# A new order of pieces in a cross-covariance attention kernel: nine stores held behind the last V load, K^T Q copies on ScalarE, last store in halves

## Chip, cores, metric

One core of a Trainium2 chip. The metric is the device time of one execution in microseconds (us). Times of before and after are medians of several runs; the profile is that of one execution. A ratio of two kernels is the mean time of one's fast runs over the mean of the other's fast runs of the same rounds, so it is not quite the ratio of the quoted medians.

## The reference

Q, K and V have the shape (8, 12, 512, 64) in float32: 96 heads of 512 tokens and 64 features.

```python
Q_norm = Q / (np.linalg.norm(Q, axis=-2, keepdims=True) + 1e-10)   # norm over the tokens
K_norm = K / (np.linalg.norm(K, axis=-2, keepdims=True) + 1e-10)
attn = np.einsum('bhnd,bhne->bhde', Q_norm, K_norm)                # 64x64 per head
attn = softmax(attn, axis=-1)
return np.einsum('bhnd,bhde->bhne', V, attn)
```

The three inputs are 37.75 MB and the output is 12.58 MB: 96 transfers of 0.5 MB.

## The kernel before

Four heads are a unit (24 units), two units a pair (12 pairs). The work is cut into pieces with short names that the text uses: `lq`, `lk`, `lv` load Q, K, V of a unit; `cq` casts Q or K to bf16 on DVE; `gr` multiplies [Q|K] with itself on PE (64 matmuls, one PSUM buffer); `sq` takes the squares out of it and `kq` copies K^T Q; `rd`, `sc`, `lg`, `ex`, `nm` make the attention matrix of a pair; `cv` casts V, `vt` transposes it on PE, `vc` copies the transpose out of PSUM; `ou` is the last product, `oc` its copy out of PSUM, `st` the store.

The program sorts these pieces itself, before it emits them. Each engine then runs its instructions in that fixed order, whatever arrives first. The sorting uses a duration and a rank that are written beside each piece:

```python
class Order:
    HOP, SLACK, QUEUE, FLIGHT = 0.15, 0.25, 8, 2.0
    def run(self):
        ...   # again and again: of the pieces that could begin first, emit the one of lowest rank
# a few of the pieces: key, {engine: booked us}, after, behind, rank
piece(("gr", u), {"PE": 1.6}, [("cq", u, 0), ("cq", u, 1), back("sq", u, 1)], [], 2, grams, u)
piece(("sq", u), {"DVE": 1.30}, [("gr", u), back("sc", s, NB["sm"])], [back("sq", u, 1)], 1, squares, u)
piece(("lv", v), {"DMA": X}, [back("cv", v, NB["v"])], [back("lv", v, 1)], v_at(v), load_v, v)
piece(("st", s, i), {"DMA": X}, [("oc", s, 2 * i), ("oc", s, 2 * i + 1)], order, v_at(2 * s + i) + ST_LAG, store, s, i)
```

```python
def grams(u):                     # PE: 64 weight loads and 64 matmuls
    g = gram[u] = ps_g.tile([128, HU, 512], F32, name="gram")
    for t in range(T):            # T = 16
        for h in range(HU):       # HU = 4
            x = qkb[u][32 * h:32 * (h + 1), t, :]
            nc.tensor.matmul(g[:, h, 0:2 * D], x, x, start=(t == 0), stop=(t == T - 1))

def squares(u):                   # DVE: squares twice, then the copy of K^T Q
    ...
    nc.vector.tensor_copy(kq[s][k], g[k, :, q])

def vtrans(s, k):                 # PE: one half of a pair's transposes
    for c in range(2):
        for j in range(J // 2):
            for r in range(2):
                t = J * c + k * (J // 2) + j
                nc.tensor.transpose(ps[r * D:(r + 1) * D, c, j, :], vb[2 * s + r][:, t, :], identb)
```

All loads and stores are issued in order by one queue (SP).

## Time and profile before

| | before |
|---|---|
| time, median | 135.4 us (135.18 to 135.93) |
| span of the profiled execution | 133.0 us |
| busy: PE, DVE, ACT, POOL | 83.4, 94.5, 64.9, 56.1 us |
| PE instructions in the profile | 2496 matmuls and 2496 weight loads |
| rate of the transfers until 110 us | 408 to 411 GB/s |

The prediction below shows the slices, stretches and waits. Two more lines of the page matter later. I did not use them for the prediction. The first belongs to the table of transfer queues (packets, MB, share): it is the queue that brings instructions, not data. The second is from the waits (total us, times, longest): PE stood still in the middle of its product while nothing that the profile knows was missing ("issue").

```profile
q8 instruction: 19, 0.31, 0.9%
```

```profile
PE gram L170 <- issue: 8.2, 6, 2.0
```

### The profile page before, as it was taken

The page shows a single profiled execution, that of the slowest core. Times are in us where ns is not written, and L with a number is a line of the kernel's source. Part 1 is how long each engine was busy: PE and PEld are TensorE (multiplying, and loading weights), DVE is VectorE, ACT ScalarE, POOL GpSimd, SP SyncE. Part 2 cuts the span into 40 slices and gives each one's busy share as a digit, 9 for nine tenths or more (in the row PEclk, how much of TensorE's full clock was granted, in tenths as well). Part 3 has the DMA queues.
Part 4 walks back from the last instruction along what each step waited for, and adds up shares of the span by engine and source line. Part 5 has one row for each costly group of instructions (what it writes and reads, how often), then busy time and mean ns, then how long its engine had stood idle before and what let it go on. Part 6 is the DMA issues. An engine that isn't in the chain of part 4 may idle for free.

```text
span 133.0 us, 5673 instructions
## 1 busy us (share of the span) xinstructions
PE 83.4 (63%) x2496; PEld 70.0 (53%) x2496; DVE 94.5 (71%) x186; ACT 64.9 (49%) x164; POOL 56.1 (42%) x55
## 2 busy tenths in 40 slices
PE   0145587585669944666859957459745956486550
PEld 0134486464457833654749845457634845485330
DVE  2477958899799469667754787467987679879800
ACT  0000056555632957155552885464857475269570
POOL 3000642869527328373066059064361378172000
PEclk9999999999655799777555699855999599959955
DMA  4999999999999999999999999999999999972976
GB/s 143 394 424 413 406 410 405 409 408 411 402 406 412 409 411 412 411 410 416 405 414 405 421 408 406 410 418 405 409 416 407 417 411 392 338 288 87 373 278 225
DMA packets 16921, 50.70 MB, mean 381 GB/s; under 512 B 1536, under 2 KB 1536, under 8 KB 16896
## 3 DMA queue, kind: packets, MB, share of 16 engines
q1 hardware_dynamic: 16896, 50.34, 95.9%
q8 instruction: 19, 0.31, 0.9%
q14 instruction: 6, 0.05, 0.1%
HBM read 37.75 MB, written 12.58 MB: 378 GB/s over the span
## 4 chain that ended last, share of the span: by engine, by line
DMA 41%; PE 19%; DVE 14%; issue 9%; ACT 8%; POOL 4%; SPq 1%; DVEq 1%; POOLq 1%; ACTq 0%
DMA v<-in_V_dram 15%; DMA qk<-in_K_dram 12%; PE gram L170 9%; DMA qk<-in_Q_dram 8%; DMA out_dram<-so 7%; PE po L250 4%; ACT vt L135 4%; DVE scr L180 4%; DVE qkb L158 3%; PE vps L231 3%; POOL r L194 3%; PE lg L203 2%; ACT so L135 2%; DVE so L137 2%; DVE kq L185 2%
## 5 line engine op out<-in xcount | busy, mean ns | idle before, releaser
L170 PE MATMUL gram<-qkb 32*128 32x128 bf16 x1536 | 37.7, 263 | 26.3 <-DVE qkb L158 15.0
L170 PEld LDWEIGHTS <-qkb 32*128 32x128 bf16 x1536 | 31.1, 117 | 31.5 <-DVE qkb L158 17.1
L194 POOL TENSOR_TENSOR r<-n,mhalf 128x8 f32<-128x8 f32 x12 | 22.3, 1858 | 42.4 <-DVE n L189 38.1
L158 DVE CAST qkb<-qk 128x1024 bf16<-128x1024 f32 x48 | 34.8, 761 | 7.4 <-DMA qk<-in_Q_dram 6.4
L135 ACT COPY vt<-vps 128x1024 bf16<-128x1024 bf16 (+1 forms) x26 | 28.2, 1089 | 13.0 <-PE vps L231 9.6
L139 POOL TENSOR_SCALAR vb<-v 128x1024 bf16<-128x1024 f32 x22 | 24.7, 1126 | 20.5 <-DMA v<-in_V_dram 20.2
L180 DVE SCALAR_TENSOR_TENSOR scr<-gram,eye 64x256 f32<-64x256 f32 x48 | 20.2, 422 | 17.7 <-PE gram L170 17.1
L135 ACT COPY so<-po 128x512 f32<-128x512 f32 x41 | 23.0, 592 | 17.3 <-PE po L250 17.1
L250 PE MATMUL po<-ab,vt 128*64 128x128 bf16 x384 | 21.6, 256 | 11.3 <-ACT vt L135 7.6
L250 PEld LDWEIGHTS <-vt 128*64 128x64 bf16 x384 | 15.7, 130 | 15.9 <-ACT vt L135 9.2
L210 ACT ACTIVATE ex<-lg,r 128x64 f32<-128x64 f32 x48 | 14.4, 313 | 15.9 <-PE lg L204 15.9
L231 PE MATMUL vps<-identb,vb 128*64 128x128 bf16 x384 | 20.1, 261 | 2.9 <-issue 1.8
L231 PEld LDWEIGHTS <-vb 128*64 128x64 bf16 x384 | 16.3, 137 | 4.3 <-issue 2.3
L203 PE MATMUL lg<-eye,kqs 64*64 64x64 f32 x96 | 10.3, 264 | 4.9 <-POOL kqs L196 4.9
L203 PEld LDWEIGHTS lg<-eye,kqs 64*64 64x64 f32 x96 | 8.4, 169 | 6.8 <-POOL kqs L196 5.9
L219 DVE TENSOR_TENSOR ab<-ex,rinv 64x256 bf16<-64x256 f32 x24 | 10.7, 446 | 0.6
L204 PE MATMUL lg<-eye,kqs 64*64 64x64 f32 x96 | 10.3, 264 | 0.0
L185 DVE COPY kq<-gram 64x256 f32<-64x256 f32 x24 | 10.1, 419 | 0.3
L210 ACT ACT_TABLE_LOAD x1 | 1.3, 1283 | 18.2 <-PE lg L204 18.2
L210 ACT ACTIVATION_READ_ACCUMULATOR ex<-lg,r 128x1 f32 x48 | 9.8, 205 | 0.0
L189 DVE TENSOR_REDUCE n<-scr 128x8 f32<-128x512 f32 x12 | 8.2, 687 | 0.4
L196 POOL TENSOR_TENSOR kqs<-kq,r 128x256 f32<-128x256 f32 x12 | 8.0, 669 | 0.9
(15 smaller groups left out, 23.2 us busy)
## 6 DMA issues: line engine op xcount, KB each, us to landing
qk<-in_Q_dram SPq DMA_DIRECT2D x24, 512.0 KB, 10.1
qk<-in_K_dram SPq DMA_DIRECT2D x24, 512.0 KB, 10.1
v<-in_V_dram SPq DMA_DIRECT2D x24, 512.0 KB, 10.1
out_dram<-so SPq DMA_DIRECT2D x24, 512.0 KB, 8.4
```

What stands on the lines that cost most here:

```text
L135: nc.scalar.copy(o, i)
L139: nc.gpsimd.tensor_scalar(out=o, in0=i, scalar1=1.0, scalar2=0.0, op0=ALU.mult, op1=ALU.add)
L158: nc.vector.tensor_copy(qkb[u][:, :, y * D:(y + 1) * D], qk32[u][:, y])
L170: nc.tensor.matmul(g[:, h, 0:2 * D], x, x, start=(t == 0), stop=(t == T - 1))
L180: nc.vector.scalar_tensor_tensor(out=scr[s][half, HU * (x ^ r):HU * (x ^ r) + HU], in0=g[half, :, half], scalar=1e-20, in1=eye2[half, None ...
L185: nc.vector.tensor_copy(kq[s][k], g[k, :, q])
L194: nc.gpsimd.tensor_tensor(out=t_, in0=n2, in1=mhalf, op=ALU.pow)
L203: nc.tensor.matmul(l[LO, h, :], kqs[s][HI, h, :], eye2[HI])
L210: nc.scalar.activation(e[:, h, :], lg[s][:, h, :], AF.Exp, scale=r8[s][:, h:h + 1], accum_out=z[:, h:h + 1])
L219: nc.vector.tensor_tensor(out=a[half, :, half], in0=e[half], in1=ri[half, :, None].to_broadcast([D, HU, D]), op=ALU.mult,)
L231: nc.tensor.transpose(ps[r * D:(r + 1) * D, c, j, :], vb[2 * s + r][:, t, :], identb)
L250: nc.tensor.matmul(po[s, x][e * D:(e + 1) * D, j].rearrange("p r d -> p (r d)"), w, ab[s][:, h, :])
```

## The change

The intent: the transfers are full until 110 us and then run dry, because stores that wait for outputs stand in front of the last V loads. So put Q and K loads earlier, issue all V loads without being held, and leave nine stores and the two halves of the last one to be drained at the end. To make the Q/K part faster, the K^T Q copy becomes a piece of its own that may run on ACT.

```diff
-    NB = dict(qk=5, v=4, vb=6, qkb=3, vt=3, so=8, sm=2, ab=3)
+    NB = dict(qk=6, v=5, vb=4, qkb=3, vt=3, so=8, sm=2, ab=3)
...
+    def cross(eng, u):
+        ...
-        nc.vector.tensor_copy(kq[s][k], g[k, :, q])
+        copy(eng, kq[s][k], gram[u][k, :, q])
...
-    X = 1.27
-    QK_PACE, V_FROM, V_PACE, ST_LAG = 0.76, 0.10, 0.80, 0.10
+    X = 1.29
+    KQ_BIAS, CV_BIAS, VC_BIAS, OC_BIAS, CQ_RANK = 1, 0, 0, 0, 5
+    QK_PACE, V_FROM, V_PACE, ST_LAG = 0.7, 0.15, 0.75, 0.3
...
-        piece(("gr", u), {"PE": 1.6}, ...
-        piece(("sq", u), {"DVE": 1.30}, ...
+        piece(("gr", u), {"PE": 1.75}, ... back("sq", u, 1), back("kq", u, 1)], ...
+        piece(("sq", u), {"DVE": 0.86}, ...
+        piece(("kq", u), {"ACT": 0.43, "DVE": (0.43, KQ_BIAS)}, ...
...   # booked durations of casts, V copies and output copies are changed by a few per cent
+            if (s, i) == (S - 1, 1):     # the last store in two halves
+                piece(("sh", s, i), {"DMA": 0.67}, [("oc", s, 2)], ..., store, s, i, 0)
+                piece(("st", s, i), {"DMA": 0.67}, [("oc", s, 3)], ..., store, s, i, 1)
```

The emitted order has all 24 K^T Q copies on ACT, three V casts on DVE (two before), and the last V load as the 86th transfer with only stores behind it.

More of the change, by code (lines that the diff above doesn't have):

```diff
@@ L149, in load_v, with store @@
         nc.sync.dma_start(out=v32[u], in_=Vu[u * 128:(u + 1) * 128])
-    def store(s, i):
-        nc.sync.dma_start(out=Of[s, i], in_=so[s, i])
+    def store(s, i, k=None):
+        rows = slice(None) if k is None else slice(k * (J // 2), (k + 1) * (J // 2))
+        o = Of[s, i].rearrange("p r (j d) -> p r j d", d=D)
+        nc.sync.dma_start(out=o[:, :, rows], in_=so[s, i][:, :, rows])
     def cast_qk(u, x):
@@ L176, in squares @@
             scr[s] = small.tile([128, 2 * HU, D], F32, name="scr")
-            kq[s] = small.tile([128, HU, D], F32, name="kq")
         g = gram[u]
@@ L183, in squares @@
             )
+    def cross(eng, u):
+        s, r = divmod(u, 2)
+        if r == 0:
+            kq[s] = small.tile([128, HU, D], F32, name="kq")
         k, q = (HI, LO) if r == 0 else (LO, HI)
-        nc.vector.tensor_copy(kq[s][k], g[k, :, q])
+        copy(eng, kq[s][k], gram[u][k, :, q])
     def sums(s):
@@ L281, in piece @@
     def piece(key, engines, after, behind, rank, fn, *args):
-        if key[0] in ("cv", "vc", "oc"):
+        if key[0] in ("cv", "vc", "oc", "kq"):
             plan.add(key, engines, after, behind, rank, lambda eng: fn(eng, *args))
@@ L295 @@
         piece(("lk", u), {"DMA": X}, free, [("lq", u)], at, load_qk, u, 1)
-        piece(("cq", u, 0), {"DVE": 0.70}, [("lq", u), back("gr", u, NB["qkb"])], [back("cq", u, 1, 1)], 10 + u, cast_qk, u, 0)
-        piece(("cq", u, 1), {"DVE": 0.70}, [("lk", u)], [("cq", u, 0)], 10 + u, cast_qk, u, 1)
-        piece(("gr", u), {"PE": 1.6}, [("cq", u, 0), ("cq", u, 1), back("sq", u, 1)], [], 2, grams, u)
-        piece(("sq", u), {"DVE": 1.30}, [("gr", u), back("sc", s, NB["sm"])], [back("sq", u, 1)], 1, squares, u)
+        piece(("cq", u, 0), {"DVE": 0.72}, [("lq", u), back("gr", u, NB["qkb"])], [back("cq", u, 1, 1)], CQ_RANK + 0.001 * u, cast_qk, u, 0)
+        piece(("cq", u, 1), {"DVE": 0.72}, [("lk", u)], [("cq", u, 0)], CQ_RANK + 0.001 * u, cast_qk, u, 1)
+        piece(("gr", u), {"PE": 1.75}, [("cq", u, 0), ("cq", u, 1), back("sq", u, 1), back("kq", u, 1)], [], 2, grams, u)
+        piece(("sq", u), {"DVE": 0.86}, [("gr", u), back("rd", s, NB["sm"])], [back("sq", u, 1)], 1, squares, u)
+        piece(("kq", u), {"ACT": 0.43, "DVE": (0.43, KQ_BIAS)}, [("gr", u), back("sc", s, NB["sm"])], [back("kq", u, 1)], 1.1, cross, u)
     for s in range(S):
         piece(("rd", s), {"DVE": 0.69}, [("sq", 2 * s), ("sq", 2 * s + 1), back("sc", s, NB["sm"])], [], 1, sums, s)
-        piece(("sc", s), {"POOL": 2.4}, [("rd", s), back("lg", s, NB["sm"]), back("ex", s, NB["sm"])], [], 1, powers, s)
+        piece(("sc", s), {"POOL": 2.5}, [("rd", s), ("kq", 2 * s), ("kq", 2 * s + 1), back("lg", s, NB["sm"]), back("ex", s, NB["sm"])], [], 1, powers, s)
         piece(("lg", s), {"PE": 0.8}, [("sc", s), back("ex", s, 1)], [], 1, logits, s)
@@ L308 @@
         piece(("lv", v), {"DMA": X}, [back("cv", v, NB["v"])], [back("lv", v, 1)], v_at(v), load_v, v)
-        piece(("cv", v), {"POOL": 1.05, "DVE": (0.7, 0.2)} if s >= BOTH else {"POOL": 1.05},
+        piece(("cv", v), {"POOL": 1.08, "DVE": (0.72, CV_BIAS)} if s >= BOTH else {"POOL": 1.08},
               [("lv", v), back("vt", v // 2, NB["vb"] // 2, 1)], [back("cv", v, 1)], 3 + 0.01 * v, cast_v, v)
@@ L316 @@
             if t:
-                wait = [("vc", s - 1, k, c) for c in halves] if s > TAIL else [("sq", U - 1)]
+                wait = [("vc", s - 1, k, c) for c in halves] if s > TAIL else [("sq", U - 1), ("kq", U - 1)]
             else:
@@ L323 @@
             order = [("vc", s, *vcopies[n - 1])] if n else []
-            piece(("vc", s, k, c), {"ACT": 0.66, "DVE": 0.60} if s >= BOTH else {"ACT": 1.31},
+            piece(("vc", s, k, c), {"ACT": 0.74, "DVE": (0.74, VC_BIAS)} if s >= BOTH else {"ACT": 1.31},
                   [("vt", s, k)] + [back("ou", s, NB["vt"], x) for x in range(4)], order, 3 + 0.01 * s, vcopy, s, k, c)
@@ L328 @@
             n = 4 * (s - TAIL if t else s) + x - 2
-            wait = [("oc", n // 4 + (TAIL if t else 0), n % 4)] if n >= 0 else [("sq", U - 1)] if t else []
+            wait = [("oc", n // 4 + (TAIL if t else 0), n % 4)] if n >= 0 else [("sq", U - 1), ("kq", U - 1)] if t else []
             order = [("ou", s, x - 1) if x else back("ou", s, 1, 3)]
@@ L334 @@
             order = [("oc", s, x - 1) if x else back("oc", s, 1, 3)]
-            piece(("oc", s, x), {"ACT": 0.6, "DVE": (0.6, 0.2)} if s >= BOTH else {"ACT": 0.6}, [("ou", s, x)] + free, order, 2 + 0.01 * s, ocopy, s, x)
+            piece(("oc", s, x), {"ACT": 0.6, "DVE": (0.68, OC_BIAS)} if s >= BOTH else {"ACT": 0.6}, [("ou", s, x)] + free, order, 2 + 0.01 * s, ocopy, s, x)
         for i in range(2):
             order = [("st", s, 0) if i else back("st", s, 1, 1)]
-            piece(("st", s, i), {"DMA": X}, [("oc", s, 2 * i), ("oc", s, 2 * i + 1)], order, v_at(2 * s + i) + ST_LAG, store, s, i)
+            if (s, i) == (S - 1, 1):
+                piece(("sh", s, i), {"DMA": 0.67}, [("oc", s, 2)], order, v_at(2 * s + i) + ST_LAG, store, s, i, 0)
+                piece(("st", s, i), {"DMA": 0.67}, [("oc", s, 3)], [("sh", s, i)], v_at(2 * s + i) + ST_LAG, store, s, i, 1)
+            else:
+                piece(("st", s, i), {"DMA": X}, [("oc", s, 2 * i), ("oc", s, 2 * i + 1)], order, v_at(2 * s + i) + ST_LAG, store, s, i)
     for emit, eng in plan.run():
```

## The prediction

> **What bounds the kernel now.** I read the utilisation slices of the page first, then busy time by stretches, then the waits of the transfer queue, then the timeline of that queue and of the engines at the end.
>
> ```profile
> span 133.0 us, 5673 instructions
> DVE  2477958899799469667754787467987679879800
> DMA  4999999999999999999999999999999999972976
> GB/s 143 394 424 413 406 410 405 409 408 411 402 406 412 409 411 412 411 410 416 405 414 405 421 408 406 410 418 405 409 416 407 417 411 392 338 288 87 373 278 225
> ```
>
> No compute engine is full for long; the transfers are: from slice 2 to slice 33 they move 400 to 420 GB/s without a hole. The only hole is near the end (288, 87, 373, 278, 225). So the kernel is bound by transfers for 110 us, and by something else in the last 23 us. Busy time by stretches (columns: stretch, its length, then PE, PEld, DVE, ACT, POOL busy, PE clock, share of the DMA engines, GB/s):
>
> ```profile
> 66.00:90.00 24.00, 16.41 (x494) 13.82 (x493) 15.19 (x32) 14.01 (x31) 12.00 (x10) 0.71 1.03 411
> 90.00:110.00 20.00, 14.21 (x462) 11.89 (x456) 16.02 (x32) 12.31 (x30) 8.83 (x9) 0.85 1.03 411
> 110.00:119.00 9.00, 5.86 (x172) 5.04 (x174) 7.80 (x16) 4.44 (x13) 4.73 (x5) 0.85 0.96 360
> 119.00:122.00 3.00, 2.47 (x68) 2.25 (x65) 2.61 (x5) 2.46 (x7) 1.52 (x2) 0.87 0.07 27
> 123.00:128.00 5.00, 2.77 (x56) 2.15 (x56) 2.85 (x7) 3.37 (x7) 0.00 (x0) 0.86 1.01 371
> 129.00:131.70 2.70, 0.00 (x0) 0.00 (x0) 0.00 (x0) 0.33 (x1) 0.00 (x0) 0.50 1.01 379
> ```
>
> Between 119 and 122 us almost nothing moves while DVE, PE and ACT are above 80% busy: they compute the outputs that the stores need. From 123 us only stores are left, and they run at 371 to 379 GB/s with the engines full. Why did the transfers run dry? The timeline of the queue from 104 us:
>
> ```profile
> 105.57 0.40 SPq L152 DMA_DIRECT2D out_dram<-so  x1
> 106.05 0.42 SPq L149 DMA_DIRECT2D v<-in_V_dram  x1
> 108.34 4.27 SPq L152 DMA_DIRECT2D out_dram<-so  x2
> 112.72 0.42 SPq L149 DMA_DIRECT2D v<-in_V_dram  x1
> 113.28 16.45 SPq L152 DMA_DIRECT2D out_dram<-so  x7
> ```
>
> All transfers are issued in order by one queue. Two stores stood ahead of the last V load and waited for their outputs (the group runs from 108.34 to 112.61), so the last V load was issued only at 112.72. The queue's waits for the last 33 us say the same:
>
> ```profile
> SPq L152 <- ACT so L135: 14.1, 5, 7.1
> SPq L152 <- DVE so L137: 5.2, 3, 3.4
> ```
>
> The stores wait 19.3 us there for their outputs. That V load took 7.1 us to land (119.8), DVE cast it at 120.77, and the last output copy ended only at 129.32:
>
> ```profile
> 128.74 0.58 ACT L135 COPY so<-po 128x512 f32<-128x512 f32 x1 [0.24 <-PE po L250]
> ```
>
> **What the Trainium skill says.** (1) "DMA: Bandwidth & Descriptors", section "Issuing engines are not separate DMA queues", has all transfers on the same 16 engines, whatever issues them; the section "Anatomy of one DMA" says that a semaphore wait happens on the issuing sequencer, before dispatch. The trace agrees: the load behind the waiting stores does not start. Its specifications give a ceiling of 435 GB/s and a limit of about 358 for a core out of HBM; this trace runs at 408 to 411, above the second, so I use the measured rate. (2) The same "Anatomy" gives about 2 us fixed per transfer, mostly the receipt of the last write. Here the last store's data stop at 131.7 and the span ends at 133.0: 1.3 us, which I keep. (3) "Perfetto Trace Analysis", section "Optimizing Scalar/DVE Operations": about 125 ns overhead for DVE on PSUM against 51 for ScalarE, and work may be moved to ScalarE when DVE is saturated. The trace agrees in sign: the 128x512 copy out of PSUM takes 687 ns on DVE and 592 on ACT. (4) "SBUF — State Buffer", section "SBUF: two separate sides": DVE and GpSimd take a port pair exclusively, and the loser blocks. The 128x1024 cast on DVE took 0.69 us at 100.35 with no GpSimd work beside it, 1.14 us at 112.79 beside a GpSimd cast that ran to 113.38; the average over 48 is 761 ns.
>
> **The change, part by part.**
>
> *Order of the transfers.* The instruction listing of the changed kernel shows no early V loads: twelve Q and K loads come first, stores begin at the 43rd transfer instead of the 30th, the last K load is the 73rd instead of the 81st or so, and from the 74th on a V load and a store alternate. The last V load is the 86th with nothing but stores behind it: nine whole ones and two halves, 5.24 MB. Before, seven stood behind it, but the load itself was held up.
>
> When will it land? In the full stretch of before, a queued transfer is issued whenever the one eight places ahead lands. From the 18th (17.15 us) to the 52nd (60.55 us) that is 43.4/34 = 1.277 us for each. So number n lands at about 17.15 + 1.277 x (n - 10). Number 86 is issued when number 78 lands, at 104.0, and lands at 114.2: 8.7 us ahead of its issue and 5.6 us ahead of its landing before.
>
> The total: at 110.0 us the kernel before has 6.50 MB left (its rate of 282 GB/s over the last 23 us). The changed one has the same bytes left if it too is never starved until then. Of these, 5.24 MB are stores with nothing beside them, at 379 GB/s: 13.8 us. The other 1.26 MB go at 410: 3.1 us. Data end at 126.9, the span at 128.2. That is 4.8 us less than 133.0, and it is the floor of this theory.
>
> *Do the outputs come in time?* After the last V load lands (114.2): a cast on POOL 1.05, transposes 0.65, two half copies of 0.74 on each of ACT and DVE in parallel (two rounds, 1.5), product 0.4, then four output copies on ACT one after another, 4 x 0.59 = 2.4, and some six hand-overs at 0.05 to 0.1: 6.5 us, so 120.7. Meanwhile eight earlier stores have 8 x 0.524 MB / 379 GB/s = 11.1 us of moving to do, until 125.3. The last pair's outputs have some 3 us to spare, if the earlier pairs are not late. Work in that stretch: each pair of V units needs 4 x 0.73 for vt copies and 4 x 0.6 for outputs = 5.3 us over two engines, 2.7 each, against 5.1 us between the landings of two pairs when loads and stores alternate. That fits.
>
> *K^T Q copies.* 24 copies of 419 ns, 10.1 us, leave DVE, all of them for ACT by the listing. DVE's work per Q/K unit was two casts 1.52, two squares 0.84, the copy 0.42, and half a pair's reduction, reciprocal and normalisation (0.69 + 0.17 + 0.89)/2 = 0.88: 3.66 us. It becomes 3.24. A unit's Q, K and V transfers take 3 x 1.277 = 3.83 us, so DVE falls from 96% to 85% of its supply in the stretch without stores. That is what allows the Q/K units to be put first. ACT gets 24 x about 0.43 (the program's own booking; I have no ACT row of this shape) = 10.3 us: 64.9 becomes some 75, 58% of a 128 us span. Per unit: vt copy 1.31, outputs 1.18, half the exponentials 0.65, K^T Q 0.43 = 3.57 against 3.83. Tight but not over. None of this counts in the sum; it only keeps the transfers fed.
>
> *Last store in halves.* The first half may start an output copy (0.6 us) earlier. With a queue of stores still draining, the last output is ready before its turn, so I give it 0. Smaller rows in it might cost 0.1.
>
> *Buffers.* One more for Q/K and for V, two fewer for cast V. They cost no time of their own.
>
> Sum: 128.2, plus 0.6 for outputs or orders that come a little late in places I can't see = 128.8 span. The measured time is 2.4 us above the span (135.39 - 133.0), so 131.2.
>
> **Rivals.** *A: compute remains late.* The last 23 us before show compute, not transfers, as the limit: pairs came out at 4 to 5 us each while Q/K work was still going on DVE. If DVE, still 84 of 128 us and stalled on the product in PSUM (17.1 us of its waits are for PE), can't finish Q/K work by about 105, the held stores come late again: half the gain goes, 132.5 to 134. For it: DVE's idle time was already made of waits that don't shrink. Against: Q/K loads come eight places (10 us) earlier and it has 10 us less to do. *B: ACT becomes the bound.* The one product buffer is now released by DVE and ACT; a copy of 0.43 us stuck behind a vt copy of 1.31 us would delay PE. At worst about 1 us for each of several units, 132 to 135. Against: eight transfers in flight hide waits up to 10 us. *C: pure stores run slower than 379.* Some 1 us stretches near 113 to 115 us move only 337; at that rate 5.24 MB take 15.5 us, 1.7 us more: 132.3. *D: the output buffers fill:* stores held too long occupy all eight output buffers and stop ACT; 132 to 133. Against: the eighth store before the end of the hold lands by about 113, before the last pair needs its buffer.
>
> **Range and chances.** The floor is 130.6 (128.2 + 2.4). Rival A or C in part gives 132 to 133.4; I take 129.9 to 133.4, with 131.2 as the time. Faster by 2% means under 132.7: 0.80. Within 2%: 0.17. Slower would need a long starvation early on: 0.03.
>
> **What would show it.** Right: the hole (27 GB/s at 119 to 122) gone, the last V load issued near 104, pure stores from about 114 on at some 375 GB/s, last output copy two or more us before the data end, span near 128.8; DVE near 84 us and ACT near 75. Wrong: the queue still waits for ACT's outputs with the transfers idle behind (A, B), or full engines at under 350 GB/s (C), or holes before 110 us.

## The result

142.75 us (141.25 to 143.46, 4 runs, the longest of them slow) against 135.4 us (4 runs): ratio 1.050, 95% interval 1.040 to 1.060. The changed kernel is slower by 5%, where 3% faster was predicted. The profile taken then was of a slow run; a later repeat (experiment 15, median 141.64 us, ratio 1.050) gave a profile of the fast state, of a run of 142.7 us with a span of 140.9 us. The lines shown here are from that one; the slow one reads the same.

The slices of the changed kernel:

```profile
span 140.9 us, 5710 instructions
DVE  2376789889754496798658839084399557745410
DMA  4999999999999999999999999999997898436936
GB/s 174 330 420 415 408 413 402 412 405 406 409 402 409 406 411 403 410 409 411 416 409 417 412 409 415 407 418 408 408 395 256 262 357 345 155 149 221 345 120 211
```

The hole did not close. It begins earlier (the 31st slice, from 106 us) and is longer. The stretches (columns as in the prediction):

```profile
66.00:90.00 24.00, 16.83 (x512) 14.37 (x512) 15.61 (x28) 15.03 (x36) 13.75 (x10) 0.72 1.03 412
90.00:110.00 20.00, 13.10 (x378) 11.03 (x377) 13.49 (x26) 11.55 (x38) 8.71 (x8) 0.74 0.97 378
119.00:122.00 3.00, 2.29 (x40) 2.05 (x40) 2.26 (x5) 0.27 (x1) 0.16 (x1) 0.50 0.38 145
128.00:138.00 10.00, 6.38 (x96) 4.95 (x92) 3.44 (x5) 5.64 (x10) 0.00 (x0) 0.50 0.69 257
```

The queue and the last output copy:

```profile
99.04 0.39 SPq L154 DMA_DIRECT2D out_dram<-so  x1
106.97 0.33 SPq L149 DMA_DIRECT2D v<-in_V_dram  x1
...
111.54 1.71 SPq L149 DMA_DIRECT2D v<-in_V_dram  x1
113.83 23.66 SPq L154 DMA_DIRECT2D out_dram<-so  x11
```

```profile
136.38 0.59 ACT L135 COPY so<-po 128x512 f32<-128x512 f32 x1 [0.21 <-PE po L257]
```

The V loads were not free to run ahead either: one was issued only at 106.97, the last during the 1.71 us from 111.54. From 92 us on the queue waited 8.7 us for a V cast on DVE before it could issue V loads, and 19.1 us for output copies on ACT and DVE (total us, times, longest):

```profile
SPq L154 <- ACT so L135: 12.8, 8, 3.5
SPq L149 <- DVE vb L137: 8.7, 2, 6.7
SPq L154 <- DVE so L137: 6.3, 4, 4.6
```

The last copy ended at 136.97, where 120.7 was predicted.

**The Q/K part is late.** The start of each unit's squares on DVE shows the pace. The last ones:

```profile
116.09 0.86 DVE L180 SCALAR_TENSOR_TENSOR scr<-gram,eye 64x256 f32<-64x256 f32 x2 [0.44 <-PE gram L170]
```

before, and after

```profile
112.01 0.86 DVE L181 SCALAR_TENSOR_TENSOR scr<-gram,eye 64x256 f32<-64x256 f32 x2 [1.41 <-PE gram L172]
```

Q and K arrived about ten us earlier, but the last squares came only 4.1 us earlier. In return, 36 of the 48 output copies were done by then before, and 29 now. These counts follow from the fixed orders: every run of each order that I counted has the same. The kernel's own plan books the last squares at 112.1 us before and at 100.7 us after. So before is 4.9 us behind its plan there (they end at 116.95), the changed kernel 12.2 us (112.87).

**PE stands still.** The changed kernel's longest waits of PE (total us, times, longest):

```profile
PE gram L172 <- DVE qkb L160: 13.5, 6, 5.9
PE gram L172 <- issue: 12.2, 7, 2.9
...
PE po L257 <- issue: 2.9, 3, 1.5
...
PE vps L238 <- issue: 1.6, 2, 1.2
```

With one of 1.0 us in the attention product (`lg`), 17.7 us in 13 stalls are put down to nothing that the profile shows (11.8 in 10 before). They lie within groups of matmuls whose inputs were all there.

The moments of these stalls tell more. In the timeline they end at 30.43, 36.62, 42.67, 48.86, 55.06, 61.26, 67.45, 73.37, 79.29, 85.22, 91.14, 97.33 and 103.63 us. I cut the time at these moments (columns: stretch, length, PE busy and matmuls, clock, share of the DMA engines, GB/s):

```profile
30.42:36.61 6.19, 3.33 (x128) 1.00 1.03 408
36.61:42.66 6.05, 3.16 (x127) 0.91 1.02 404
42.66:48.85 6.19, 4.81 (x128) 0.50 1.03 407
48.85:55.05 6.20, 5.68 (x128) 0.50 1.03 407
...
73.36:79.28 5.92, 5.06 (x128) 0.50 1.04 413
...
85.21:91.13 5.92, 2.84 (x128) 1.00 1.04 413
91.13:97.32 6.19, 4.02 (x128) 0.63 1.03 411
97.32:103.62 6.30, 5.84 (x128) 0.55 1.04 411
```

Twelve times in a row PE got through 128 matmuls (once 127 in the record) in 5.9 to 6.3 us, whether it was busy for 2.8 or 5.8 of them and whatever its clock. With their weight loads these are 256 instructions. The Trainium skill, "Runtime: NRT & Kernel Launch", section "Instruction fetch mechanics", says that each engine's instructions are refilled in blocks of 16 KiB, 256 instructions, by a transfer queue that the sequencer drives, and calls the cost mostly hidden. The trace agrees with the block (19 packets, 0.31 MB, is 16 KB each) and not with the hiding: while the data transfers are full, a block comes each 6.1 us or so, and PE can run no faster. The kernel before gets its blocks at the same pace:

```profile
42.11:48.30 6.19, 4.44 (x128) 0.79 1.04 413
```

The trace also keeps the time of each of these 19 transfers of 16,384 bytes; no view of the profile prints them, so the following is read from the packed trace itself, with blocks of 128 matmuls counted from the stall that ended at 30.43 us. From 34.04 to 101.17 us they start 5.9 to 6.3 us apart. In that stretch a block's transfer starts 3.5 to 3.8 us after PE began on the block before it, takes 0.9 to 1.1 us, and PE goes on with the new block 1.3 to 1.5 us after its end: together about 6.1 us. When the data transfers thin out, so does the first of these three: the transfers at 111.33 and 117.80 us start 1.2 and 1.0 us after PE began on the block before.

That makes a bound which I had not seen. PE had run 479 matmuls at 30.42 us. The other 2017 are 15.8 blocks; at 6.1 us each that is 96 us, so about 127 us for all of PE's work as long as the transfers stay full. This is an estimate from the rows above. A plan that wants PE done with the last pair at 120 us can't be met with 2496 matmuls.

### The profile page after: what moved, and what is told of

Read it like the earlier page. It is cut to its first block, busy times and chain, and to the rows that moved or that the text cites. A ratio compares the mean times of both kernels' runs of the same rounds, so it can differ in the third digit from the quotient of the medians.

```text
span 141.7 us, 5710 instructions
## 1 busy us (share of the span) xinstructions
PE 87.4 (62%) x2496; PEld 74.5 (53%) x2496; DVE 88.6 (63%) x163; ACT 72.5 (51%) x188; POOL 59.7 (42%) x54
## 4 chain that ended last, share of the span: by engine, by line
DMA 58%; PE 14%; DVE 12%; issue 5%; ACT 5%; SPq 3%; DVEq 0%
DMA qk<-in_Q_dram 31%; DMA qk<-in_K_dram 21%; DMA v<-in_V_dram 7%; PE gram L172 5%; PE po L257 5%; DVE qkb L160 4%; DVE vt L137 3%; PE vps L238 3%; SPq L145 3%; ACT vt L135 3%; ACT so L135 2%; DVE scr L181 2%; DVE n L196 1%; DVE ab L226 1%; PE lg L210 1%
## 5 line engine op out<-in xcount | busy, mean ns | idle before, releaser
L201 POOL TENSOR_TENSOR r<-n,mhalf 128x8 f32<-128x8 f32 x12 | 25.1, 2094 | 54.3 <-DVE n L196 48.7
L160 DVE CAST qkb<-qk 128x1024 bf16<-128x1024 f32 x48 | 36.5, 792 | 7.2 <-DMA qk<-in_Q_dram 5.7
L257 PE MATMUL po<-ab,vt 128*64 128x128 bf16 x384 | 24.0, 279 | 12.2 <-DVE vt L137 3.9
L135 ACT COPY vt<-vps 128x1024 bf16<-128x1024 bf16 (+1 forms) x24 | 27.0, 1126 | 6.2 <-PE vps L238 3.2
L135 ACT COPY kq<-gram 64x256 f32<-64x256 f32 x24 | 8.8, 367 | 40.5 <-DVE scr L181 20.6
L257 PEld LDWEIGHTS <-vt 128*64 128x64 bf16 x384 | 17.6, 144 | 17.5 <-issue 6.3
L238 PE MATMUL vps<-identb,vb 128*64 128x128 bf16 x384 | 21.2, 274 | 1.4 <-issue 1.4
L238 PEld LDWEIGHTS <-vb 128*64 128x64 bf16 x384 | 18.1, 149 | 1.9 <-issue 1.7
L210 PEld LDWEIGHTS lg<-eye,kqs 64*64 64x64 f32 x96 | 8.7, 173 | 6.1 <-POOL kqs L203 5.3
L137 DVE COPY vt<-vps 128x512 bf16<-128x512 bf16 x8 | 5.8, 726 | 5.6 <-ACT vt L135 5.4
L211 PEld LDWEIGHTS lg<-eye,kqs 64*64 64x64 f32 x96 | 8.7, 173 | 0.7 <-issue 0.7
```

What stands on the lines that cost most here:

```text
L135: nc.scalar.copy(o, i)
L160: nc.vector.tensor_copy(qkb[u][:, :, y * D:(y + 1) * D], qk32[u][:, y])
L201: nc.gpsimd.tensor_tensor(out=t_, in0=n2, in1=mhalf, op=ALU.pow)
L210: nc.tensor.matmul(l[LO, h, :], kqs[s][HI, h, :], eye2[HI])
L211: nc.tensor.matmul(l[HI, h, :], kqs[s][LO, h, :], eye2[LO])
L257: nc.tensor.matmul(po[s, x][e * D:(e + 1) * D, j].rearrange("p r d -> p (r d)"), w, ab[s][:, h, :])
```

## The experiments

Seventeen runs. "Order kept" means that the emitted order of each engine is that of the named kernel, save the pieces that move.

### 1 and 2. K^T Q copies back on DVE; V casts on POOL (changed kernel, order kept)

```diff
-        return [(self.pieces[key][4], eng) for ...]
+        return [(self.pieces[key][4], "DVE" if key[0] == "kq" else eng) for ...]     # 1
+        return [(self.pieces[key][4], "POOL" if key[0] == "cv" else eng) for ...]    # 2
```

> The changed kernel (142.75 us), every order kept, but all 24 K^T Q copies run on DVE again at the same places. Theory 1 (ACT is coupled to the Q/K chain: each copy waits for the squares, and ACT's V copies queue behind it): time falls to 135 to 138 and ACT's waits of some 40 us before these copies go. Theory 2 (V casts on DVE stand behind late Q/K work, so V loads are issued late and the transfers run dry): stays at 141 to 143, V loads still issued as late as 107 to 114. Theory 3 (the fixed order books the Q/K stage too short, which slips whatever engine copies): 140 to 144, the last squares still at 112 or later.

> The changed kernel, every order kept, but the three V casts that were put on DVE run on POOL. Theory 2: the last V load is issued near 104 instead of 113.8, the hole of the transfers after 94 us is gone, time 135 to 139. Theory 1 and theory 3: V loads may go out earlier, but the outputs are as late as before, 141 to 143.

Measured: 141.05 us (ratio 1.036 [1.028, 1.044]) and 140.57 us (1.038 [1.033, 1.044]), both correct. Each takes back about one of the five per cent. In 2 the V loads wait for casts on POOL instead (one at 107.51, the last at about 111). In 1 the last squares still began at 112.1 us. Theories 1 and 2 name small costs; neither is the cause.

### 3. K^T Q copies on ACT in the kernel before (order kept)

```diff
-        nc.vector.tensor_copy(kq[s][k], g[k, :, q])
+        nc.scalar.copy(kq[s][k], g[k, :, q])
```

> The kernel before (135.4 us), every order kept, with the K^T Q copies on ACT at the same places. Theory 1: slower by 2 to 6 us (138 to 141), with ACT waiting in front of the copies. Theories 2 and 3: within 1.5 us of 135.4 either way.

Measured: 137.39 us, ratio 1.016 [1.012, 1.020]: 2 us slower. That lies below the 138 to 141 us of theory 1 and above the 1.5 us of the others, so it decides between none of them. On ACT the copy never ran beside the squares: in the trace of the changed kernel it starts after them, or they after it, each time.

### 4. The transfers alone, in the changed order

```diff
     for emit, eng in plan.run():
-        emit(eng)
+        if eng == "DMA":
+            emit(eng)                 # stores send a tile of zeros
```

> Only the transfers of the changed kernel in its order, with no computation; the stores send a tile of zeros (output wrong on purpose). My floor of 130.6 us for this order: 130 to 131.5, stores alone at about 379 GB/s at the end. If the order of transfers or the pure stores themselves cost the time (rival C of the prediction), 133 or more.

Measured: 129.49 us (2 runs), output wrong on purpose. The order of the transfers is as good as predicted, even better: the stores alone ran at full rate, not at 379 GB/s.

```profile
106.00:119.00 13.00, 0.00 (x0) 0.00 (x0) 1.00 1.04 411
```

(columns: DVE and POOL busy, clock, share of the DMA engines, GB/s). Rival C falls, and the loss lies in the computation.

### 5 and 6. The computation with few loads

```diff
     def load_qk(u, x):
+        if u >= NB["qk"]:
+            qk32[u] = qk32[u - NB["qk"]]      # compute on old data; load_v in the same way
+            return
```

> The changed kernel without transfers to wait for: only the first six Q/K units and five V units are loaded, later units compute on these tiles again (output wrong on purpose); every order, all computation and all stores are kept. If the computation in its fixed order is the bound (theory 3), the time hardly falls: 132 to 139. If late V loads and starved transfers set the end (theory 2), it falls to 120 or less.

> The same for the kernel before. Theory 3: its computation alone takes 124 to 131, less than that of the changed kernel by 5 or more, and a unit still takes some 4.8 us on average. If the transfers bound it, 115 or less.

Measured: 129.75 us for the changed kernel and 127.17 us for the one before (2 runs each). For the changed kernel that is lower than theory 3 wanted (132 to 139) and higher than theory 2 wanted (120 or less). The kernel before lies within the 124 to 131 us of theory 3, but only 2.6 us below the changed one, where 5 or more were expected, and a unit takes 4.4 us in it, not 4.8. So the fixed computation takes as long as the transfers alone (129.49 us), and the two disturb each other. What they disturb is PE. All its unexplained stalls are gone in both (0 us, against 17.7 and 11.8), with the same 2496 matmuls. From 30 to 60 us, first without loads, then the changed kernel:

```profile
30.00:60.00 30.00, 21.32 (x816) 0.87 0.25 91
```

```profile
30.00:60.00 30.00, 21.70 (x638) 0.72 1.03 408
```

PE runs 816 matmuls in place of 638 in the same time, with the transfers at 91 GB/s in place of 408. This run also takes away waits for data, so it does not show the instructions alone. Its 19 instruction blocks tell more (packed trace again): from the third on, a block's transfer starts 0.7 us (median) after PE began on the block before, in place of 3.5 to 3.8 us. The moment at which PE begins a block is counted by matmuls here and can be off by a microsecond or two.

### 7 and 8. Half of the Q/K products

```diff
-        for t in range(T):
+        for t in range(0, T, 2):
```

> The changed kernel with half of the Q/K products (8 of 16 row groups, output wrong on purpose): PE has 768 matmuls and some 19 us less to do, half of that on the chain product, squares, copy, next product. If PE's time in this chain is what makes a unit take 4.8 us: 142.75 falls to 131 to 136. If DVE or the transfers hold the chain: 139 or more.

> The same for the kernel before. If PE binds it too: 135.4 falls to 130 to 132, near the floor of the transfers. If not: 134 or more.

Measured: 130.88 us (changed) and 132.98 us (before), 2 runs each, no unexplained stalls in either. With less to do on PE, the changed order is the faster one, by 2 us, and comes to 1.4 us of its transfers alone. Its last squares end at 101.5 us in place of 112.9, where the plan books 100.7; in the order before they end at 115.2 in place of 116.95. So the change does what it was meant to, once PE keeps up. The profiled runs of 7 and 8 had mean clocks of 0.784 and 0.752, like the changed kernel's 0.757: a low clock alone does not make the loss. But half the products are both half the time and half the instructions; the next pair takes these apart.

### 9 and 10. Half the instructions, or half the columns

9 has 768 product matmuls of 256 columns; 10 has all 1536, of which 1344 have 64 columns. Both outputs are wrong on purpose. (A first form of 10 was refused by the checks and never ran; the record has nothing of it.)

```diff
-        for t in range(T):
+        for t in range(0, T, 2):                                        # 9
-                nc.tensor.matmul(g[:, h, 0:2 * D], x, x, ...)
+                nc.tensor.matmul(g[:, h, 0:4 * D], x, y, ...)           # 9: y has the columns of t and t + 1
+                nc.tensor.matmul(g[:, h, 0:n], x, x[:, 0:n], ...)       # 10: n = 128 for the first and last t, else 64
```

> The changed kernel with half of the Q/K product instructions, each with 256 moving columns in place of 128 (output wrong on purpose): PE streams as many columns as before but has 768 matmuls and weight loads fewer. If PE is late because its instructions arrive late under full transfers (theory 4: its unexplained stalls of 1 to 3 us within a product group, some 18 us in all, are gone in the runs with fewer instructions or fewer transfers), the time falls nearly as far as with half of the products (130.9): 131 to 135. If PE's streaming time is what counts: 139 or more.

> The changed kernel with all 1536 Q/K product instructions, most with 64 moving columns in place of 128 (output wrong on purpose). Theory 4: stays at 139 to 143, the stalls are still there. If PE's streaming time counts: 131 to 136.

Measured: 131.1 us for half the instructions with all columns, 140.82 us for all the instructions with half the columns (2 runs each). What counts is the number of instructions, not the streaming: PE is busy longer with the products of 9 (33.6 us) than with those of 10 (27.5 us), and 9 is the faster by ten us.

```profile
L173 PE MATMUL gram<-qkb 32*128 32x256 bf16 x768 | 33.6, 328 | 24.1 <-DVE qkb L160 18.1
L173 PE MATMUL gram<-qkb 32*128 32x64 bf16 (+1 forms) x1536 | 27.5, 236 | 31.4 <-issue 14.1
```

Weight loads are halved along with the matmuls in 9, so these two runs do not tell one kind of instruction from the other; run 5 has all of both and no stall. The instruction queue follows the count: 13 packets in 7, 8 and 9, 18 in the runs with 2304 matmuls below, 19 in every other run that computes. Run 9 has no unexplained stall; run 10 has 18.9 us of them, at the same six-microsecond pace:

```profile
42.27 0.52 PE L173 MATMUL gram<-qkb 32*128 32x64 bf16 x42 [2.00 <-issue]
48.74 0.40 PE L173 MATMUL gram<-qkb 32*128 32x64 bf16 x10 [3.54 <-issue]
54.94 0.47 PE L258 MATMUL po<-ab,vt 128*64 128x128 bf16 x10 [1.39 <-issue]
```

### 11 and 12. Fewer instructions with a correct result

Two units' cast V in one tile, so that one transpose serves both: 2304 matmuls in place of 2496.

```diff
-                for r in range(2):
-                    nc.tensor.transpose(ps[r * D:(r + 1) * D, c, j, :], vb[2 * s + r][:, t, :], identb)
+                nc.tensor.transpose(ps[:, c, j, :], vb[s][:, t, :], identb)    # vb[s] is [128, T, 2 * D]
```

> The kernel before with the cast V of two units in one tile, so that one transpose of 128 columns takes the place of two of 64: 192 matmuls and 192 weight loads fewer, a correct result. Theory 4: faster by 1 to 3 us (132.5 to 134.5), fewer stalls of PE. If instructions don't count: within 0.7 us of 135.4.

> The same edit on the changed kernel. Theory 4: faster by 2 to 5 us (138 to 141), as its order has no slack for the stalls. Otherwise 141.5 to 143.

Measured: before 134.29 us (ratio 0.993 [0.990, 0.996]), changed 134.9 us (0.990 [0.980, 1.000]), both correct. On the changed kernel 8% fewer matmuls are worth some 8 us by the ratios of fast runs (1.050 and 0.990; only two of the four runs of 12 count as fast), more than I expected; on the kernel before about 1 us, at the lower end (its stalls fall to 5.0 us). The stalls are not gone in 12 (15.4 us): it still gets one block in 5.9 to 6.2 us, but has less to run. Its profiled run has a granted clock of 0.892 against 0.757, and that run was the fastest of its four; I can't say how much of the 8 us is the clock.

### 13 and 14. The same with K^T Q copies on DVE, and with V casts on POOL too

The edits of 1, and of 1 and 2 together, on 12.

> The changed kernel with merged transposes (134.9), order kept, K^T Q copies on DVE again. If ACT's coupling to the Q/K chain costs 1 to 2 us beside the stalls: 132.5 to 134. If it helped once the stalls are fewer: 135.5 to 137.

> The same, and the three V casts on POOL as well. If both costs add as they did in the first experiments (1.7 and 2.2 us on the changed kernel): 131 to 133, the best correct version. If they only mattered because everything was late: 134 to 136.

Measured: 137.58 us (1.022 [1.014, 1.031]) and 134.63 us (0.993 [0.990, 0.996]), both correct. By the ratios of fast runs, copies on DVE alone now cost 3.2% where they gained 1.4% in experiment 1. 13 lies 0.6 us above the second of its two cases, 14 within the second of its two (134 to 136): these two moves do not add. I have no cause for the sign, but the traces hold a warning. The unexplained stalls are 4.0 us in 13 and 5.4 us in 14, against 15.4 in 12, and 13 is still the slowest of the three. In 13 PE waits longer for POOL before `lg` (9.9 us, 3.5 in 12) and for the squares (7.0, 3.3), and its instruction blocks still come each 6.1 us (11 intervals from 34.22 us on). So the sum of unexplained stalls does not rank versions: the same supply may hide behind other waits. No version beats the kernel before by more than about 1%.

### 15. The changed kernel again

> The changed kernel unedited, on the chip of the other two. 141 to 143.5; in the fast state the last squares at 111 to 113 us and stalls of PE of 15 to 19 us in all.

Measured: 141.64 us (1.050 [1.044, 1.056]). Its profile is the one shown above: last squares from 112.0 us, 17.7 us of stalls.

### 16 and 17. Loads in halves

```diff
+        for p in range(2):            # each load in two transfers, rows of 2 KB in place of 4 KB
+            nc.sync.dma_start(out=qk32[u][:, x ^ (u % 2), p * 8:(p + 1) * 8], in_=...)
```

> The changed kernel with every load of Q, K and V in two halves of 2 KB rows. If instruction blocks wait behind the bytes in flight (or behind long rows): the 6.19 us per 256 instructions fall to 3 to 4, PE's stalls go and the time falls to 130 to 134. If the rate has another cause: still about 6.1 us per block, 140 to 144 us.

> The same on the kernel before. In the first case 132 to 134 (half the products gave 133.0), else 134.5 to 137.

Measured: 139.99 us (1.027 [1.022, 1.032]) and 139.67 us (1.035 [1.031, 1.039]), both correct. Neither expectation holds. Blocks came somewhat faster, if not evenly; these are four consecutive stretches of run 16, of 128 matmuls each:

```profile
63.82:70.57 6.75, 3.15 (x128) 0.90 1.05 396
70.57:75.94 5.37, 5.06 (x128) 0.50 1.05 399
75.94:81.86 5.92, 3.36 (x128) 0.99 1.02 375
81.86:87.23 5.37, 2.84 (x128) 1.00 1.05 396
```

From 34.14 to 101.66 us a block came each 5.6 us on average (12 intervals), in place of 6.1, and the stalls fell to 10.0 us (2.1 in 17). But loads in such rows are slower: 367 GB/s from 30 to 60 us in place of 408, and the data queue was then busy for 99.2% of 16 engines' span. So the changed kernel became bound by transfers. The rate of instruction blocks moved along with how the data are cut, but what sets it remains open.

## Why the prediction was wrong

- **The floor of the transfers** (128.2 us span) was right, and a little high: 127.5 measured. The term that was off is the rate of stores alone, 379 GB/s taken from stretches in which stores trickled in; 408 to 411 measured. Two smaller slips: the 2.4 us between span and time compare a median with one profiled run, which itself took 134.82 us for a span of 133.0, so 1.8; and by its own times the last outputs had 4.6 us to spare (125.3 - 120.7), not some 3. The 2 us per transfer that it quotes stand in a section on transfers issued from GpSimd; those here are issued by SP, and it used the 1.3 us of the trace.
- **"None of this counts in the sum; it only keeps the transfers fed"** is the step that failed. I divided DVE's busy time by the supply of data (3.24 of 3.83 us) and took it that the Q/K part would follow its loads. It does not: in the changed kernel a unit takes 4.7 us on average from unit 6 to 23 ((112.0 - 31.4)/17), before 5.0 ((116.1 - 31.6)/17). In that stretch PE gets 128 matmuls in about 6.1 us, and I had no term for that. The Q/K part is a chain (cast, product, squares, copy, next product), so PE's stalls lengthen it directly. With half the instructions and all the columns (experiment 9), in the same order, a unit takes 4.1 us and the last squares end at 102.0. (DVE's own work was also a little under-booked: busy for 90.2 us where 84 was predicted, the casts at 826 ns in place of 761.)
- **"Do the outputs come in time?"** fell with it. The order puts V work behind Q/K work on every engine, so V copies and casts wait for late squares, V buffers come free late, and V loads go out late: predicted 104.0, measured about 112. 19 of 48 output copies were left when the Q/K part ended, against 12 before, and they took 24.1 us (112.87 to 136.97) against 12.4 (116.95 to 129.32). That longer tail belongs to the order: it takes 22.5 us in experiments 7 and 9 too. So the change gives away 11.7 us at the end and had to win them in the Q/K part. It won 4.1; the other 7.6 us are nearly all of the difference of the spans (7.9). By then the stalls are few; the tail is a chain of PE, ACT and DVE with PE at a clock of 0.50 for most of it.
- **Why the kernel before suffers less.** It gets blocks at the same pace (128 matmuls in 6.2 us from 42 to 48 us) and has 11.8 us of stalls. Half the products take 2 us off it (132.98) and 11 to 12 off the changed kernel (130.88). The traces show where: its last squares come only 1.7 us earlier then, those of the changed kernel 11.4. The order before books them at 112.1 in any case, so it loses little when PE can't go faster.
- **Rival A** had the direction (compute late, the held stores late again), but named DVE and gave 132.5 to 134. DVE is busy for 64% of the span; it waits for PE. **Rival B**, ACT, is worth about 1%, with an open sign. **C** is refuted. **D** was not what the queue waited for: it waited for output copies and V casts.
- **The chances** put 0.03 on slower. "It would need a long starvation early on" was wrong: a steady shortage of instructions needs no hole in the data transfers, which look perfect until 103 us.
- The cost of the halved last store was never measured alone.

What stays open: why a block's transfer starts only 3.5 to 3.8 us after PE begins the block before while data transfers are full, which is the larger part of the 6.1 us; how much of the loss goes through PE's clock, which differed from run to run (0.704 to 0.895 in the profiled ones, with no fixed relation to the stalls); and why experiment 13 is slower than 12.

## What to carry to other kernels

When unexplained stalls of an engine come at even intervals, count its instructions between them: equal counts in equal times are a supply limit, and then fewer and larger instructions help where shorter ones don't (131.1 against 140.8 us here). A fixed order that has no slack against its booked durations turns a small lag of one engine into late buffers and late loads; before trusting a new order, compare its booked times with the trace of the old one. An engine's busy share says nothing on this: PE was 63% busy before and after.

## What the Trainium skill lacked or had wrong

- "Runtime: NRT & Kernel Launch", section "Instruction fetch mechanics": says that the cost of a 16 KiB block is mostly hidden. Here PE gets one block of 256 instructions per 5.9 to 6.3 us while data move at 404 to 413 GB/s, twelve times in a row, and stalls for 17.7 us; without most of the loads, 0 us.
- "Perfetto Trace Analysis": the parts that I read on finding the bound speak of busy shares, waits and repeating gaps, which are put down to too few buffers; the count of instructions between stalls is missing. It told apart what busy time couldn't.
- "DMA: Bandwidth & Descriptors", the limit of about 358 GB/s for a core out of HBM stands in its specifications without a condition: 408 to 411 here with one core running. This agrees with the page's own section "Measured", which calls 358 the share when both cores of a pair stream; so the row is to be read with that section. No page gives a rate for loads with rows of 2 KB beside rows of 4 KB on this chip: loads with rows of 2 KB ran at 367 to 401 GB/s in place of 407 to 412, while stores with rows of the same size, alone, ran at 411.
